# Layer A's output projection on half-precision parts with scanned scales

## The chip, the cores and the metric

The kernel runs on one core of a Trainium2 chip. Its engines have a queue of instructions each: TensorE (PE in the profile, its weight loads apart as PEld), VectorE (DVE), ScalarE (ACT), GpSimd (POOL), and SyncE (SP), which issues the transfers. The metric is the device time of one execution in microseconds; the time before is the median of 3 runs.

## The reference

Two layers of gated attention over 2,048 prompt rows and 64 sample rows (2,112 together, called tokens below), width 1,024. Layer A attends in a window of 192 keys with 16 query heads on 2 key heads and a sink per head; layer B has 16 heads and 576 keys.

```python
def gated_attention_layer(x_p, x_s, ck, cv, norm_g, w_in, q_g, k_g, w_out,
                          n_heads, n_kv, past_chunks, bias_fn, sinks):
    qp, kp, vp, gp = project(x_p, norm_g, w_in, q_g, k_g, n_heads, n_kv)
    op = prompt_band_attention(qp, kp, vp, past_chunks, bias_fn, sinks)
    y_p = x_p + (op * jax.nn.silu(gp)) @ w_out
    ...
for i in range(DEPTH):
    if i % 2 == 0:
        x_p, x_s, k_a_p, v_a_p, k_a_s, v_a_s = gated_attention_layer(...)
    else:
        x_p, x_s, k_b_p, v_b_p, k_b_s, v_b_s = gated_attention_layer(...)
```

`project` normalizes the rows, multiplies by one matrix for q, k, v and the gate, and normalizes q and k per head. What the change touches is `(op * silu(gp)) @ w_out` of the first layer: a product of 2,112 x 1,024 by 1,024 x 1,024.

## The kernel before, in words

**Parts.** A float32 product is made of two parts of each factor, a high one and a low one (what the high one leaves): the kernel multiplies high by high, high by low and low by high, three matmuls. In layer A's output projection the parts are in the format float32r; in layer B's they are half precision (f16), for which both factors are first multiplied by powers of two so that their size fits. Such a scale comes of the largest absolute value of the weights or a bound on the activations. `scan` (L175 to L188) loads pieces of weights (L187) and reduces each to a maximum per partition (L178); it does this for layer B's input weights and output weights only.

**Layer A's attention** (`layer_a`) is a pipeline over 68 items: four groups of four heads (`qd`) by 17 tiles of 128 tokens. An item makes scores, their maxima and exponentials (L1347 on ACT), casts P (L1361) to `values`, transposes it, two heads by DMA and two on TensorE (these are split by L981 on ACT and L982 on DVE, to `ph` and `pl`), multiplies it with the values (L1408), and evacuates (L1495), multiplies by the gate and stores the result (`oga`). Between these steps `filler.to(mark)` puts matmuls of other work on TensorE: first the input projection of the next head group (L758 to L760), and, when that is used up, from about the 59th item, the first units of the output projection.

**Layer A's output projection** is `output_jobs(0, half, ...)`, for two halves of 512 output columns; each half has 8 units of 264 tokens, and a unit 4 blocks (`m`) of 128 columns by 8 chunks (`k`) of 128 rows of the weights. For each `m` and `k` there are three matmuls of 128x264: L2059 (high weights, high activations), L2060 (high, low), L2061 (low, high), 512 of each in all. The block's sum in `pj` (PSUM) is added to the residual by DVE (L2069, the combine), and the rows' squares are summed for the next layer's normalization (`sum_squares`).

The weights of a half come in eight transfers of 128x512 to raw buffers `wraw` (3 of them); the split of each is a cast on ACT to `wh` (L537) and a subtraction on DVE to `wl` (L538). There are 12 buffers `wh` and 12 `wl`. The splits are put in a background list and worked off ahead of their use. The activations of a unit come by four transfers of 128x528 to `xraw` (4 buffers); each is cast by ACT (L639), and POOL makes its low part (L640):

```python
cast = nc.scalar.copy(hi, rv)
nc.gpsimd.tensor_tensor(lo, rv, wide(hi), op=ALU.subtract)
```

High and low parts take four of the seven buffers `xx` for a unit. A unit's activations are prefetched while the unit before it runs. Half 0's units also load one scan each (`scan(j)`).

**What sets the order.** TensorE's order is written out: the program's text with the filler's marks. The order on the other engines is set by a scheduler which sees dependences, buffers and priorities, so that an instruction that becomes possible earlier, or a buffer that is used otherwise, can move others past each other on ACT, DVE, POOL and SP. Each engine then works off its list in order.

**After it.** Layer B (`layer_b`) begins with its input projection and the first items of its attention: copies of q between partitions (L1628 on SP's queue), scores (L1683, L1684), transposes of P (L1748). Its output projection (L2304 to L2308) is half precision with the same 128x264 matmuls.

## Time and the profile before

| | us |
|---|---|
| runs | 2069.28, 2071.61, 2078.48 |
| median | 2071.61 |
| the profiled execution | 2078.12 |
| its span, from the first to the last instruction | 2076.2 |
| layer A's attention up to the last eight items (from the start) | 120 to 616 |
| these eight items, mixed with the output projection | 616 to 686 |
| the rest of layer A's output projection | 686 to 855 |
| layer B | 855 to the end |

The profile's times are counted from the start of the span of one execution. A row of a group gives the line, the engine, the operation, output and input with their shapes, the count, then busy time and the mean of one in ns, and the idle time before them with what ended it. A row of the timeline gives start, duration, and in brackets the idle time before it and its releaser. A row of the windows gives the stretch, its length, then busy time (and count) of PE, PEld, DVE, ACT and POOL, the granted clock, the share of the DMA engines and GB/s.

### The profile page before, as it was taken

The numbers are of one execution on the slowest core, as the hardware profiler recorded it, in microseconds if no ns is written. First come the engines' busy times: TensorE is split into PE (matmuls) and PEld (weight loads), VectorE is DVE, ScalarE is ACT, GpSimd is POOL, SyncE is SP. The second block draws the span as 40 slices with busy tenths as digits, with TensorE's granted clock in tenths as the row PEclk, the third lists the DMA queues.
The fourth block names the chain that finished last, engine by engine and source line by source line (L and its number), as shares of the span: only waits on it lengthen the run. The fifth ranks groups of instructions, "written<-read, shape, count | busy, mean of one in ns | idle before, by whom it ended". The sixth has DMA issues, their size and how long they took to land.

```text
span 2076.2 us, 40598 instructions
## 1 busy us (share of the span) xinstructions
PE 1985.5 (96%) x12718; PEld 1418.1 (68%) x12718; DVE 1432.5 (69%) x4093; ACT 1436.6 (69%) x3568; POOL 1182.6 (57%) x1561
## 2 busy tenths in 40 slices
PE   7899999999999999989999999999999999999899
PEld 6777777777888999745555555555555555557788
DVE  7666767767667555677767676676766767678673
ACT  6877888777788333367768777787867868678430
POOL 5665565544446445577556565665756656566540
PEclk9999999999999999999999999999999999999999
DMA  8877887899766766899889688797997978698753
GB/s 258 255 209 228 221 212 191 236 217 255 194 177 172 214 209 197 281 232 226 226 173 242 168 204 219 174 239 176 200 217 170 233 158 188 149 194 199 200 163 105
DMA packets 600216, 424.64 MB, mean 205 GB/s; under 512 B 403952, under 2 KB 531328, under 8 KB 599968
## 3 DMA queue, kind: packets, MB, share of 16 engines
q1 hardware_dynamic: 600000, 422.06, 80.1%
q8 instruction: 100, 1.64, 0.3%
q14 instruction: 116, 0.95, 0.1%
HBM read 253.14 MB, written 73.43 MB: 157 GB/s over the span
## 4 chain that ended last, share of the span: by engine, by line
PE 50%; DVE 10%; ACT 6%; DMA 5%; issue 5%; POOL 3%; SPq 0%; ACTq 0%; POOLq 0%; DVEq 0%
PE pj L758 9%; PE pj L760 9%; PE pj L759 9%; PE o L1847 4%; PE sb L1683 2%; PE pj L2059 2%; PE pj L2061 2%; PE pj L2060 2%; DMA pt<-values 2%; PE sb L1684 2%; PE pj L2304 2%; PE pj L2308 2%; PE pj L2307 2%; DVE p L1687 1%; PE tp L1011 1%
## 5 line engine op out<-in xcount | busy, mean ns | idle before, releaser
L758 PE MATMUL pj<-wh,xx 128*128 128x512 f16 (+2 forms) x1648 | 643.0, 390 | 17.7 <-DVE pa L852 6.0
L760 PE MATMUL pj<-wh,xx 128*128 128x512 f16 (+2 forms) x1648 | 625.0, 379 | 0.0
L1740 POOL TENSOR_TENSOR values<-p,values 128x640 f16<-128x640 f32 (+4 forms) x256 | 328.4, 1283 | 206.3 <-ACT values L1739 201.9
L759 PE MATMUL pj<-wh,xx 128*128 128x512 f16 x1024 | 388.7, 380 | 1.3 <-DVE wh L545 1.3
L1699 ACT ACTIVATE p<-p,nm 128x640 f32<-128x640 f32 (+5 forms) x264 | 199.6, 756 | 181.3 <-DVE nm L1692 147.7
L1687 DVE CUSTOM_DVE_ANT_0 p<-sb,BT 128x640 f32<-128x640 f32 (+5 forms) x272 | 196.5, 722 | 145.0 <-PE sb L1684 122.3
L640 POOL TENSOR_TENSOR xx<-xraw,xx 128x528 fp32r<-128x528 f32 (+4 forms) x144 | 186.1, 1312 | 96.8 <-ACT xx L639 81.4
L759 PE MATMUL pj<-wl,xx 128*128 128x512 f32 (+1 forms) x624 | 236.1, 378 | 3.0 <-DVE wl L545 3.0
L849 POOL TENSOR_TENSOR f<-f,mhalf 128x4 f32<-128x4 f32 x182 | 187.2, 1028 | 12.1
L1500 POOL TENSOR_TENSOR o<-gt,o 128x256 f32<-128x256 f32 (+1 forms) x132 | 105.7, 801 | 142.0 <-ACT p L1347 71.5
L760 PEld LDWEIGHTS <-xx 128*128 128x128 f16 x1024 | 100.3, 98 | 122.8 <-issue 2.4
L1347 ACT ACTIVATE p<-p,nm 128x257 f32<-128x257 f32 (+2 forms) x272 | 134.4, 496 | 67.3 <-DVE nm L1336 35.3
L1739 ACT CAST values<-p 128x640 f16<-128x640 f32 (+4 forms) x256 | 168.2, 657 | 13.8 <-DMA pt<-values 7.8
L759 PEld LDWEIGHTS <-xx 128*128 128x128 f16 x1024 | 100.3, 98 | 84.5 <-issue 4.9
L758 PEld LDWEIGHTS <-xx 128*128 128x128 f16 x1024 | 100.2, 98 | 82.8 <-ACT sq L827 1.4
L2059 PE MATMUL pj<-xx,wh 128*128 128x264 f32 x512 | 148.4, 290 | 5.3 <-DVE res L2069 2.3
L1847 PEld LDWEIGHTS <-values 128*128 128x128 f16 x1344 | 123.3, 98 | 43.3 <-issue 4.1
L1847 PE MATMUL o<-pt,values 128*128 128x256 f16 (+1 forms) x1344 | 143.7, 255 | 5.9 <-DMA pt<-values 5.9
L2061 PE MATMUL pj<-xx,wl 128*128 128x264 f32 x512 | 145.0, 283 | 0.9 <-DVE wl L538 0.9
L2060 PE MATMUL pj<-xx,wh 128*128 128x264 f32 x512 | 145.7, 284 | 0.0
L758 PEld LDWEIGHTS pj<-wh,xx 128*128 128x128 f32 x624 | 119.7, 192 | 34.9 <-issue 4.6
L760 PEld LDWEIGHTS pj<-wh,xx 128*128 128x128 f32 x624 | 119.1, 191 | 23.3
(369 smaller groups left out, 5060.8 us busy)
## 6 DMA issues: line engine op xcount, KB each, us to landing
xx<-xsb SPq DMA_DIRECT2D x112, 512.0 KB, 4.4
xx<-xsa SPq DMA_DIRECT2D x88, 512.0 KB, 4.8
xraw<-oga SPq DMA_DIRECT2D x64, 264.0 KB, 3.6
xsa<-xx SPq DMA_DIRECT2D x32, 512.0 KB, 4.0
wl<-in_w_in_b_dram SPq DMA_DIRECT2D x64, 256.0 KB, 4.9
wraw<-in_w_in_b_dram SPq DMA_DIRECT2D x56, 256.0 KB, 3.6
xraw<-in_x_dram SPq DMA_DIRECT2D x40, 256.0 KB, 4.3
res<-in_x_dram SPq DMA_DIRECT2D x32, 264.0 KB, 2.9
```

Source lines behind the costliest of these rows:

```text
L640: nc.gpsimd.tensor_tensor(lo, rv, wide(hi), op=ALU.subtract)
L758: nc.tensor.matmul(ps[:n, :C], xh, wh, start=k == 0, stop=False)
L759: nc.tensor.matmul(ps[:n, :C], xh, wl, start=False, stop=False)
L760: nc.tensor.matmul(ps[:n, :C], xl, wh, start=False, stop=k == KC - 1)
L849: nc.gpsimd.tensor_tensor(fv, fv, mhalf[:n, :H], op=ALU.pow)
L1687: mi = nc.vector.tensor_tensor_reduce(out=p[r, :nk], in0=S[r, o : o + nk], in1=b, op0=ALU.add, op1=ALU.min, scale=1.0, scalar=3e38, accum_ ...
L1699: ex = nc.scalar.activation(p[:n, :nk], p[:n, :nk], AF.Exp, scale=-1.0, bias=it.nm[:n, c : c + 1], accum_out=it.sm[:n, c : c + 1],)
L1740: lo = nc.gpsimd.tensor_tensor(two[:, :, 1, :], pv, two[:, :, 0, :], op=ALU.subtract)
L1847: nc.tensor.matmul(it.O[:, h * T + q0 : h * T + q1_], held["VH"][:, kt, h], x, start=kt == kb and not low, stop=kt == tb and low == 1,)
L2059: nc.tensor.matmul(ps[:, :OT], wh, oh, start=k == 0, stop=False)
L2060: nc.tensor.matmul(ps[:, :OT], wh, ol, start=False, stop=False)
L2061: nc.tensor.matmul(ps[:, :OT], wl, oh, start=False, stop=k == KC - 1)
```

## The change

The projection's factors become f16 with scales. For that (1) the 16 pieces of layer A's output weights are scanned during items 20 to 51 (`scales_ahead`, `scan_source`), (2) the gate's weights of each head group, and the cached values, are reduced to maxima (`gate_top`, `load_cache`), as a bound on the activations, (3) the scales are worked out at items 56 to 58 (`first_top`, `first_across`, `first_scales`). (4) Weights are split to a pair in one buffer, of `wh` or, for the last four chunks of a half, of `wl`; half 0 puts all eight splits on the background list at once (`out`). (5) ACT makes the high part of the activations with the scale and scales the raw tile in place; POOL subtracts, and a unit takes two buffers `xx`. (6) The combine multiplies by the inverse scale.

```diff
-    most = const([P, 84], "most")
-    top = const([P, 12], "top")
-    scl = const([P, 9, 4], "scl")
+    most = const([P, 133], "most")
+    top = const([P, 15], "top")
+    scl = const([P, 10, 4], "scl")
...
     S_WO, S_OG, C_O = (scl[:, 8, i : i + 1] for i in range(3))
+    S_WOA, S_OGA, C_OA = (scl[:, 9, i : i + 1] for i in range(3))
...
     def scan_source(i):
+        if i >= 84:
+            return w_o_a[(i - 84) // 8, (i - 84) % 8 // 2, :, i % 2, :]
...
             raw = t("wraw", [P, 512], WB) if keep else t("scan", [P, 512], 1)
-            dst = raw if i < 80 else raw.rearrange("p (e c) -> p e c", e=2)
+            dst = raw if not 80 <= i < 84 else raw.rearrange("p (e c) -> p e c", e=2)
...
+    def gate_top(q, w, *ks):
+        for k in ks:
+            wt, j = w[k]
+            r = nc.vector.tensor_reduce(
+                most[:, 100 + 8 * q + k : 101 + 8 * q + k], wide(wt.h[:, j, 256:512]), axis=AX.X, op=ALU.max,
+                apply_absolute_value=True,
+            )
+            behind(r.ins, bg.anchors[r.ins.engine])
+            scanned.append(100 + 8 * q + k)
+
+    def first_top():
+        largest(12, 84, 100)
+        largest(13, 100, 132)
+        largest(14, 132, 133)
+
+    def first_across():
+        across(12, 15)
+        nc.vector.scalar_tensor_tensor(
+            row[:, 14:15], row[:, 40:41], float(D), row[:, 14:15], op0=ALU.mult, op1=ALU.max
+        )
+        e, r, o = row[:, 48:51], row[:, 52:55], row[:, 56:59]
+        powers(row[:, 12:15], e, r)
+        times(o[:, 0:1], r[:, 0:1], WO)
+        nc.vector.scalar_tensor_tensor(
+            o[:, 1:2], r[:, 1:2], OO, r[:, 2:3], op0=ALU.mult, op1=ALU.mult
+        )
+        nc.vector.scalar_tensor_tensor(
+            o[:, 2:3], e[:, 1:2], 1 / (OO * WO), e[:, 2:3], op0=ALU.mult, op1=ALU.mult
+        )
+        nc.vector.tensor_tensor(o[:, 2:3], o[:, 2:3], e[:, 0:1], op=ALU.mult)
+
+    def first_scales():
+        everywhere(9, row[:, 56:59])
...
-    def load_weights(g, *specs, scale=None):
+    def load_weights(g, *specs, scale=None, apart=False):
...
-                if scale is not None:
+                if scale is not None and not apart:
                     raw = t("wl", [P, 512], WN)
...
                 if scale is None:
                     wh, wl = (t(x, [P, J, C], WN, dt) for x in ("wh", "wl"))
                 else:
-                    both = t("wh", [P, 2, C], WN, dt)
+                    both = t("wl" if apart and i >= WN - 8 else "wh", [P, 2, C], WN, dt)
                     wh, wl = both[:, 0:1], both[:, 1:2]
...
                 hi, lo = (xh[:, :, :T], xh[:, :, T:]) if joint else (xh, xl)
                 if scale is not None:
                     cast = nc.scalar.activation(hi, rv, AF.Identity, scale=scale)
-                    nc.vector.scalar_tensor_tensor(lo, rv, scale, hi, op0=ALU.mult, op1=ALU.subtract)
+                    nc.scalar.activation(rv, rv, AF.Identity, scale=scale)
+                    nc.gpsimd.tensor_tensor(lo, rv, hi, op=ALU.subtract)
...
         load(rvv, vsrc)
+        if not both:
+            nc.vector.tensor_reduce(
+                most[:, 132:133], rv[:, :C], axis=AX.X, op=ALU.max, apply_absolute_value=True
+            )
+            scanned.append(132)
...
             self.jobs, self.n, self.gen, self.done, self.total = [], -1, None, 0.0, 0.0
-        def add(self, prefetch, weights, gen, early=3):
+        def add(self, prefetch, weights, gen, early=3, out=False):
             j = Item()
+            j.out = out
             j.prefetch, j.weights, j.gen, j.early = prefetch, weights, gen, early
             self.jobs.append(j)
 
...
                         nxt.weights()
                 for nxt in self.jobs[self.n + 2 : self.n + 4]:
                     if nxt.weights is not None and nxt is self.jobs[min(self.n + nxt.early, len(self.jobs) - 1)]:
-                        nxt.weights(WN - 8)
+                        nxt.weights(KC if nxt.out else WN - 8)
...
+        def scales_ahead(i):
+            if 20 <= i < 52 and i % 2 == 0:
+                scan(84 + (i - 20) // 2)
+            elif i == 52:
+                scan()
+            q, at = divmod(i, 17)
+            if 0 <= q < 4 and 1 <= at < 5:
+                gate_top(q, st.w[q], 2 * at - 2, 2 * at - 1)
+            if i == 56:
+                first_top()
+            elif i == 57:
+                first_across()
+            elif i == 58:
+                first_scales()
+                held["out"] = True
+
         def pipeline():
             N = len(items)
             for i in range(-3, N + 1):
...
                 if i + 3 < N:
                     end = max(items[i + 3].mark, c0 + AVG_A)
                 filler.attending = i >= 0
+                scales_ahead(i)
                 if 0 <= i < N:
                     scores(items[i])
                     if i == N - 1:
...
             if st.emit is None:
+                assert layer or held["out"]
                 (st.w,), _, st.emit = load_weights(
-                    None, ((w_o_a, w_o_b)[layer][half], 512), scale=(None, S_WO)[layer]
+                    None, ((w_o_a, w_o_b)[layer][half], 512), scale=(S_WOA, S_WO)[layer], apart=layer == 0
                 )
             st.emit(*m)
 
...
-                st.x[j] = x = load_act(og[layer], o, OT, dt=(F32R, F16)[layer], scale=(None, S_OG)[layer])
+                st.x[j] = x = load_act(og[layer], o, OT, dt=F16, scale=(S_OGA, S_OG)[layer])
                 if half == 0 and j == 0:
                     st.res = residual(0, 0)
                 return x
...
                         nc.tensor.matmul(ps[:, :OT], wl, oh, start=False, stop=k == KC - 1)
-                    if layer:
-                        nc.vector.scalar_tensor_tensor(
-                            rv[:, m % 2], ps[:, :OT], C_O, rv[:, m % 2], op0=ALU.mult, op1=ALU.add
-                        )
-                    else:
-                        nc.vector.tensor_tensor(rv[:, m % 2], ps[:, :OT], rv[:, m % 2], op=ALU.add)
+                    nc.vector.scalar_tensor_tensor(
+                        rv[:, m % 2], ps[:, :OT], (C_OA, C_O)[layer], rv[:, m % 2], op0=ALU.mult, op1=ALU.add
+                    )
+                    if not layer:
                         if half == 0 and m == 0:
                             scan(j)
                         if half and j < 2 and m % 2 == 0:
...
                     yield 3 * OT / 2400
 
             filler.total += 96 * OT / 2400
-            filler.add(prefetch, weights if j == 0 else None, gen)
+            filler.add(prefetch, weights if j == 0 else None, gen, out=half == 0)
 
         for j in range(NO):
             add_unit(j)
```

Lines after the change: L2059, L2060 and L2061 become L2121, L2122 and L2123; L537 and L538 become L571 and L572; L639 becomes L669 (high part) and L670 (in place); L640 becomes L671; L2069 becomes L2126; L178 and L187 become L181 and L190.

TensorE at the first matmuls of the output projection, before: `wh` and `wl` are the weights' parts, `xx` the activations', `values` and `ph` the operands of an item's product.

```order
L1011 MATMUL tp_9048<-ident,G_8873 128x128 x2
L2059 MATMUL pj_9081<-xx_8810,wh_8507 128x264
L2060 MATMUL pj_9081<-xx_8810,wh_8507 128x264
L2061 MATMUL pj_9081<-xx_8810,wl_8508 128x264
L1408 LDWEIGHTS values_106
L1408 MATMUL o_9085<-ph_9014,values_106 128x256
L1408 LDWEIGHTS values_106
```

And after:

```order
L1054 MATMUL tp_9142<-ident,G_8985 128x128 x2
L2121 LDWEIGHTS wh_8607
L2121 MATMUL pj_9177<-xx_8920,wh_8607 128x264
L2122 LDWEIGHTS wh_8607
L2122 MATMUL pj_9177<-xx_8920,wh_8607 128x264
L2123 LDWEIGHTS wh_8607
L2123 MATMUL pj_9177<-xx_8920,wh_8607 128x264
L1452 LDWEIGHTS values_106
L1452 MATMUL o_9181<-ph_9108,values_106 128x256
L1452 LDWEIGHTS values_106
```

The order of the matmuls is the same; each now has a weight load of its own in the list, and the low weights are in the same buffer as the high ones.

ACT around the 58th item, from the cast of the transposed P's high part (`ph`) to the evacuations of the next projection (`pa`, `pb`), before:

```order
L981 CAST ph_8749<-sa_8751 128x512
L1347 ACTIVATE p_8704,sm_8697<-p_8704,nm_8696 128x257
L639 CAST xx_8810<-xraw_8802 128x528
L1361 CAST values_106<-p_8704 128x2x256
L639 CAST xx_8813<-xraw_8804 128x528
L1279 ACTIVATE q_1900_8775<-tp_8770,qf 64x2x128 x2
L1485 ACTIVATE gt_8778<-tp_8770,sva 128x256
L783 ACTIVATE pa_8786<-pj_8744,rms_102 64x256
L783 ACTIVATE pb_8787<-pj_8744,rms_102 64x256
L639 CAST xx_8816<-xraw_8806 128x528
```

And after:

```order
L1019 CAST ph_8856<-sa_8858 128x512
L1391 ACTIVATE p_8808,sm_8801<-p_8808,nm_8800 128x257
L669 ACTIVATE xx_8920<-xraw_8912,scl 128x528
L669 ACTIVATE xx_8920<-xraw_8914,scl 128x528
L1405 CAST values_106<-p_8808 128x2x256
L669 ACTIVATE xx_8927<-xraw_8916,scl 128x528
L669 ACTIVATE xx_8927<-xraw_8918,scl 128x528
L670 ACTIVATE xraw_8912<-xraw_8912,scl 128x528
L1323 ACTIVATE q_1919_8885<-tp_8880,qf 64x2x128 x2
L1546 ACTIVATE gt_8888<-tp_8880,sva 128x256
L670 ACTIVATE xraw_8914<-xraw_8914,scl 128x528
```

Where three casts of activations (L639) stood between these rows, four scaled ones (L669) and two scalings in place (L670) stand now, in front of the cast of P (L1361, now L1405) and of the evacuations that follow.

DVE where half 0 of the projection gives way to half 1: weight splits (L538, later L572), combines (L2069, later L2126), before, at the end of half 0:

```order
L2069 TENSOR_TENSOR res_10400<-pj_10461,res_10400 128x264
L2007 TENSOR_TENSOR BT<-p_10488 128x72
L2007 TENSOR_TENSOR row_9210<-p_10488 128x192
L2069 TENSOR_TENSOR res_10492<-pj_10494,res_10492 128x264
L538 TENSOR_TENSOR wl_10431<-wraw_10136,wh_10430 128x512
L538 TENSOR_TENSOR wl_10440<-wraw_10145,wh_10439 128x512
L538 TENSOR_TENSOR wl_10447<-wraw_10158,wh_10446 128x512
L2069 TENSOR_TENSOR res_10492<-pj_10520,res_10492 128x264
L538 TENSOR_TENSOR wl_10458<-wraw_10434,wh_10457 128x512
```

And after, at the sixteenth of half 0's 32 combines:

```order
L572 SCALAR_TENSOR_TENSOR wl_10536<-wraw_10240,scl,wl_10536 128x512
L572 SCALAR_TENSOR_TENSOR wl_10544<-wraw_10248,scl,wl_10544 128x512
L2126 SCALAR_TENSOR_TENSOR res_9907<-pj_9909,scl,res_9907 128x264
L2068 TENSOR_TENSOR BT<-BT,p_9895 128x264
L181 TENSOR_REDUCE most<-scan_10092 128x1
L2070 TENSOR_TENSOR BT<-BT,p_9895 128x264
L2126 SCALAR_TENSOR_TENSOR res_9907<-pj_9952,scl,res_9907 128x264
L572 SCALAR_TENSOR_TENSOR wl_10550<-wraw_10260,scl,wl_10550 128x512
L2068 TENSOR_TENSOR BT<-p_9979 128x264
L2126 SCALAR_TENSOR_TENSOR res_9982<-pj_9984,scl,res_9982 128x264
L572 SCALAR_TENSOR_TENSOR wl_10560<-wraw_10539,scl,wl_10560 128x512
L2126 SCALAR_TENSOR_TENSOR res_9982<-pj_10010,scl,res_9982 128x264
```

The last of half 1's eight splits stands ahead of half 0's sixteenth combine, where before four of them stood about the last ones.

SP where layer B begins: the loads of x and of weights (`xraw`, `wraw`), stores (`xsb`, `out_dram`), and the first copies of q, before:

```order
L391 DMA BT<-skew 128x256
L651 DMA xsb<-xx_11910 128x2048
L620 DMA xraw_12049<-x_99 128x2x256
L1628 DMA q_2399_11967<-q_2399_11967 64x256 x2
L620 DMA xraw_12051<-x_99 128x2x256
L651 DMA xsb<-xx_11924 128x2048
L620 DMA xraw_12053<-x_99 128x2x256
L187 DMA wraw_12116<-in_w_in_b_dram 128x512
L417 DMA out_dram<-in_ck_a_rows_dram 16x512
```

And after:

```order
L428 DMA BT<-skew 128x256
L657 DMA xraw_12167<-x_99 128x2x256
L689 DMA xsb<-xx_12040 128x2048
L657 DMA xraw_12169<-x_99 128x2x256
L190 DMA wraw_12232<-in_w_in_b_dram 128x512
L454 DMA out_dram<-in_ck_a_rows_dram 16x512
L1689 DMA q_2369_12083<-q_2369_12083 64x256 x2
L1809 DMA_TRANSPOSE pt_12216<-values_11903 128x2x128
```

The first copies of q come behind five transfers that followed them before.

## The prediction

> **What bounds the kernel now.** I read the page's first two parts, then the windows by stage, then the timeline of TensorE in the stage that the change touches, and last the idle times of TensorE there.
>
> ```profile
> span 2076.2 us, 40598 instructions
> PE 1985.5 (96%) x12718; PEld 1418.1 (68%) x12718; DVE 1432.5 (69%) x4093; ACT 1436.6 (69%) x3568; POOL 1182.6 (57%) x1561
> ```
>
> TensorE is busy for 96% of the span, every other engine for 69% or less. So the time follows the number of matmuls, their spacing, and the places where TensorE waits. The stages (start and end, then busy time by engine):
>
> ```profile
> 120.00:616.00 496.00, 481.90 (x2830) 390.22 (x2829) 350.02 (x1159) 399.67 (x1099) 263.47 (x441) 0.99 0.81 212
> 616.00:686.00 70.00, 66.40 (x492) 59.90 (x491) 53.35 (x150) 57.29 (x150) 46.64 (x60) 1.00 0.70 185
> 686.00:855.00 169.00, 162.72 (x1329) 161.09 (x1328) 87.98 (x158) 56.54 (x94) 80.95 (x69) 1.00 0.69 211
> 855.00:2077.00 1222.00, 1173.66 (x7506) 722.74 (x7503) 858.66 (x2361) 834.29 (x1997) 719.97 (x887) 1.00 0.82 196
> ```
>
> The columns that matter are the first (PE), third (DVE), fourth (ACT) and the granted clock. From 120 to 616 us layer A attends; from 616 to 686 the last eight items of attention share the engines with the first units of the output projection; from 686 to 855 the projection runs alone; after that comes layer B. In the projection alone TensorE is busy for 162.72 of 169 us and ACT for a third. In the mixed stage ACT is busy for 57.29 of 70 us, nearly as full as TensorE.
>
> **The change, part by part.** First the spacing of the matmuls. The two pairs of rows are the first and last of 85 float32 matmuls in a row in the projection, and of 92 half-precision ones of the same 128x264 shape in layer B's projection:
>
> ```profile
> 719.74 0.29 PE L2060 MATMUL pj<-xx,wh 128*128 128x264 f32 x1
> ...
> 729.92 0.28 PE L2060 MATMUL pj<-xx,wh 128*128 128x264 f32 x1
> ```
>
> ```profile
> 2034.76 0.28 PE L2308 MATMUL pj<-xx,wx 128*128 128x264 f16 x1
> ...
> 2044.99 0.28 PE L2304 MATMUL pj<-xx,wx 128*128 128x264 f16 x1
> ```
>
> 84 steps in 10.18 us are 121.2 ns each; 91 steps in 10.23 us are 112.4 ns. The change gains 8.8 ns on each matmul of the projection. Lines 2059, 2060 and 2061 hold 512 each, 1536 together, so 13.5 us at most. They divide so (L2059 alone):
>
> ```profile
> 616.00:686.00 70.00, 25.41 (x84) 15.75 (x84) 1.00 0.70 185
> 686.00:855.00 169.00, 122.98 (x429) 80.42 (x429) 1.00 0.69 211
> ```
>
> 3 x 429 matmuls after 686 us gain **11.3 us**; 3 x 84 in the mixed stage would gain 2.2 us if TensorE still set the pace there. The separate weight load that each now has is in the 112.4 ns already, as the rows of layer B have it too.
>
> The Trainium skill ("TensorE: Matmul & The Clock Gate", section "Back-to-back issue gap") gives a warm gap of N/2.4 + 2.5 ns, whatever the type: 112.5 ns for 264 columns, an estimate by that page. The half-precision rows agree; the float32 rows, at 121.2 ns, do not. By the rule for both kinds this term would be nothing; the rows decide.
>
> Second, the boundary between the halves. TensorE waits there for the last weight splits:
>
> ```profile
> 756.13 0.39 PE L2059 MATMUL pj<-xx,wh 128*128 128x264 f32 x1 [1.44 <-ACT wh L537]
> 757.51 0.39 PE L2061 MATMUL pj<-xx,wl 128*128 128x264 f32 x1 [0.88 <-DVE wl L538]
> ```
>
> Since both parts of a chunk now fit one buffer, half 1 needs no buffer that half 0 still holds; the order shows all eight splits ahead of the sixteenth combine of half 0, where before the last four stand at its end. I count **2.3 us** gained, at least 0 if another wait for the same loads takes its place.
>
> Third, the mixed stage. Before, TensorE stands idle in it twice:
>
> ```profile
> 641.26 0.27 PE L1408 MATMUL o<-pl,values 128*128 128x256 f16 x1 [2.00 <-DVE pl L982]
> 647.67 0.36 PE L2059 MATMUL pj<-xx,wh 128*128 128x264 f32 x1 [1.60 <-ACT QS L1292]
> ```
>
> That is 3.6 us. The first comes from weight splits that stand ahead of pl L982 on DVE; these move some 35 us earlier, so it should go. What is late next is ACT. Its own steps, from rows of several like instructions:
>
> ```profile
> 681.17 1.66 ACT L537 CAST wh<-wraw 128x512 fp32r<-128x512 f32 x3
> 689.55 2.23 ACT L639 CAST xx<-xraw 128x528 fp32r<-128x528 f32 x4
> 1925.11 2.61 ACT L2206 ACTIVATE xx<-xraw,scl 128x528 f16<-128x528 f32 x4
> ```
>
> With the last one's duration taken off (0.62, 0.63 and 0.73 us), a weight cast steps by 0.52 us, an activation cast by 0.53 and the scaled one by 0.63. ACT now does two scaled operations for each chunk: the high part, and the chunk scaled in place. The trace has no in-place one; between the square of the same tile (0.53 or so) and a full second 0.73 I take 0.63. Moreover its queue runs further ahead: two buffers serve a unit instead of four, and between the same two marks (the copies of o that end items 59 and 67) the order has 20 casts and 20 in-place scalings against 15 casts, and 3 weight activations against 7. That adds 40 x 0.63 + 3 x 0.62 - 15 x 0.53 - 7 x 0.52 = **15.3 us** to 57.29: 72.6 us of work in a stage that lasted 70. ACT runs its queue in order, and exponentials, evacuations and parts of P stand behind the scalings.
>
> The Trainium skill ("Perfetto Trace Analysis", section "Optimizing Scalar/DVE Operations") says that about half the overhead in a profiled latency overlaps with the next instruction. The rows agree (0.73 long, 0.63 apart); adding the 40 at their length, without that rule, the stage would hold 4 us more.
>
> How much reaches TensorE is not in the trace. From below: ACT's work hides altogether, and the 3.6 us and the 2.2 us are gained, -5.8. From above: ACT keeps all its idle time, +15.3. With no idle at all it is +2.6; with the idle share of the fullest stretch,
>
> ```profile
> 640.00:650.00 10.00, 7.14 (x59) 6.76 (x59) 8.00 (x24) 9.57 (x28) 8.64 (x11) 1.00 0.77 207
> ```
>
> 96% busy, 72.6 us become 75.9, +5.9. I take the middle of these two, **+4 us**.
>
> Fourth, the scans. 16 reductions of 128x512 and one small one, 32 of 128x256 and some 25 tiny operations go to DVE, 16 loads of 256 KB to SP's queue.
>
> ```profile
> L845 DVE TENSOR_REDUCE f<-sq 128x4 f32<-128x256 f32 x182 | 75.0, 412 | 16.5 <-ACT sq L797 7.6 <-ACT sq L806 7.5
> L178 DVE TENSOR_REDUCE most<-wraw 128x1 f32<-128x512 f32 x76 | 51.5, 678 | 0.3
> L2069 DVE TENSOR_TENSOR res<-pj,res 128x264 f32<-128x264 f32 x64 | 27.3, 429 | 57.0 <-PE pj L2061 56.9
> L2296 DVE SCALAR_TENSOR_TENSOR res<-pj,scl,res 128x264 f32<-128x264 f32 x48 | 23.4, 489 | 25.4 <-PE pj L2308 25.3
> ```
>
> 17 x 0.68 + 32 x 0.41 + about 3 are 28 us of DVE. In 120:616 DVE is idle for 146 us, and the waits of TensorE on DVE are few:
>
> ```profile
> PE o L1408 <- DVE pl L982: 3.1, 7, 0.5
> ```
>
> Behind a reduction on DVE stand the score minima, and ACT's exponentials wait for those; the next matmul that needs them is an item later. Behind a scan's load on SP stand the copies of q and the transposes of P. Nearly all is covered; I take **+2 us**, with 0 and 28 as ends. The combine, 489 instead of 429 ns, 64 times, is 3.8 us of DVE beside TensorE, with 81 us of idle time to cover it: nothing. The low parts stay on POOL with the same two inputs and a half-precision output; the nearest rows are L640 itself and one that writes half precision:
>
> ```profile
> L640 POOL TENSOR_TENSOR xx<-xraw,xx 128x528 fp32r<-128x528 f32 x64 | 88.1, 1405 | 60.9 <-ACT xx L639 45.9 <-DMA x<-res 8.3 <-issue 6.4
> L1740 POOL TENSOR_TENSOR values<-p,values 128x640 f16<-128x640 f32 (+4 forms) x256 | 328.4, 1283 | 206.3 <-ACT values L1739 201.9
> ```
>
> 1405 ns for 528 columns, 1283 for 640 or fewer: by either, 64 of them change by 0 to -8 us on an engine that is idle for a third or more of both stages, so nothing for TensorE. Three transposes and one small matmul for the scales cost TensorE under 1 us, which I leave out.
>
> Fifth, layer B's start. From about its third unit every engine's order is the same row for row, so it moves as a block. Ahead of that one move matters: the first copies of q stand on SP's queue ahead of five more transfers before the change and behind them after it (the second row below is the fifth).
>
> ```profile
> 875.23 1.33 SPq L1628 DMA_DIRECT2D q<-q  x2
> ...
> 880.69 0.56 SPq L417 DMA_DIRECT2D out_dram<-in_ck_a_rows_dram  x1
> ```
>
> ```profile
> q<-q SPq DMA_DIRECT2D x218, 32.0 KB, 3.4
> ```
>
> ```profile
> 881.70 0.27 PE L1683 MATMUL sb<-KA,q 128*128 128x256 f16 x1
> ```
>
> With 3.4 us from issue to landing they came by 878.6, 3.1 us before the scores that read them. Behind 880.69 + 0.56 they would be issued 6 us later and land at 884.65, 2.95 us late, and TensorE's order is fixed, so it would wait. I take **+3 us** because I see nothing that would bring the five transfers forward; the ends are 0 (they come earlier, since some of SP's waits go) and +6 (the scores had no slack at all).
>
> The sum: -11.3 - 2.3 + 4 + 2 + 3 = **-4.6 us**. The profiled execution took 2078.1 us (span 2076.2 and 1.9 around it), so 2073.5; it lies 6.5 us above the median of the runs shown, 2071.6, so for a median I forecast **2067.0**.
>
> **The rivals.** (a) ACT's extra work hides: exponentials have several microseconds of slack between scores and transposes. For it: TensorE had only two waits in the stage. Against: 72.6 us do not fit 70. It gives -5.8 instead of +4, and 1 for the scans: -15.4, 2056. (b) ACT keeps its idle time, since each scaling lets POOL and DVE start later: +15.3 instead of +4, +6.7 in all, 2078. For it: in its group POOL waits 45.9 us for L639, which becomes the slower pair L669 and L670; against: ACT was 96% busy where it was needed. (c) Slower: the DVE reductions in attention pass into the items. Price 28 us, place 120:616. It decides once 6.6 of them reach TensorE (the 4.6 gained in all, and the 2 counted); with all of them the sum is +21.4, 2093. Against it: 146 us idle there and 3.1 us of waits. (d) The change does not give its rate: layer A's matmuls stay at 121 ns because something else paces them. Then 11.3 go, +6.7, 2078.
>
> For (d) speaks only that POOL needs 4 x 1.4 us for a unit and ACT 8 x 0.63; a unit's 96 matmuls at 112.4 ns last 10.8, so both fit.
>
> **How the numbers follow.** Forecast 0.44, (a) 0.27, (b) 0.14, (c) 0.08, (d) 0.07. Runs before range over 9 us, and 0.5%, 10.4 us, is about what a measurement here tells from no change. The forecast's own spread (ACT 0 to +8, layer B 0 to +6) is -11.6 to +2.4; with the noise of the runs a fifth of it is over 0.5% faster, with nearly all of (a): 0.35. (c) with over 17 of its 28 us, and the upper edge of (b) and (d), are over 0.5% slower: 0.10; the rest, 0.55, is within.
>
> ```profile
> 699.22 0.39 PE L2059 MATMUL pj<-xx,wh 128*128 128x264 f32 x1 [1.85 <-DVE res L2069]
> ```
>
> This wait comes of a scan on DVE and may go with (a). The range holds (a) with some noise and without it, down to 2051, and (b) and (d) up to 2082; outside are most of (c) and a little on each side.
>
> **What would show it.** Rows of 128x264 half-precision matmuls 112 ns apart from about 690 us to the start of layer B, and that stretch about 14 us shorter: first two terms. No wait of TensorE at the half's boundary: second. ACT busy over 95% in the last eight items of attention, and those items longer than before by some 4 us: third; wrong if they are shorter. Items before 616 us as long as before within 2 us: fourth. The first scores of layer B waiting some 3 us for their q: fifth. The prediction is wrong if layer B's stretch changes by more than that, or if TensorE's idle time appears behind POOL's low parts.

## The result and the profile after

| | before, us | after, us | ratio, 95% interval |
|---|---|---|---|
| first set (4 and 4 runs) | 2070.53 | 2090.24 (2089.32 to 2094.04) | 1.0091 [1.0062, 1.0119] |
| second set (23 and 6 runs) | 2072.49 | 2092.99 (2086.92 to 2094.73) | 1.0100 [1.0075, 1.0125] |
| profiled execution (span) | 2078.12 (2076.2) | 2090.94 (2088.8) | |

The change costs about 20 us; forecast was a gain of 4.6, with a range that ended at 2082. One of the 23 executions of before, 3002.85 us at a granted clock of 0.63, counts in the median and not in the ratio. The two profiled executions are only 12.8 us apart: that of before was some 6 us above its median, and the table below has before 5.4 us longer in a stretch of layer B (B 0-12) where the change alters no operation.

To see where the time went, the spans are cut at the same events in both: the copies that end an item of attention (L1495, after the change L1556) and the last matmul of layer A's projection. Each column is the length of a stretch in us. "A" stands for layer A's items, "B" for layer B's; the scales are worked out between items 55 and 59, and the third stretch is the mixed one.

| | A 0-55 | A 55-59 | A 59-66 | projection | to B 0 | B 0-12 | rest |
|---|---|---|---|---|---|---|---|
| before | 508.0 | 32.8 | 62.8 | 176.2 | 54.3 | 207.8 | 956.1 |
| after | 508.8 | 36.5 | 67.9 | 179.8 | 59.4 | 202.4 | 957.2 |
| after, second profile | 510.9 | 35.9 | 67.8 | 181.3 | 59.8 | 203.0 | 955.0 |

"Projection" runs from the last but one item's end to the last matmul. There the forecast gained 13.6 us; the profiles lose 3.6 and 5.1. The half-precision matmuls do run at the rate that was counted. The timeline of TensorE after the change, first and last of 91 in a row:

```profile
824.30 0.27 PE L2121 MATMUL pj<-xx,wh 128*128 128x264 f16 x1
...
834.43 0.28 PE L2121 MATMUL pj<-xx,wl 128*128 128x264 f16 x1
```

90 steps in 10.13 us are 112.6 ns. What goes against it are waits. TensorE's waits from 690 to 870 us (releaser, us in all, times, longest), after the change:

```profile
PE pj L2121 <- DVE res L2126: 12.1, 7, 3.9
PE o L736 <- DVE BT L2070: 3.0, 3, 1.5
PE o L736 <- DVE scrow L221: 1.9, 1, 1.9
```

The same view of before, from 683 to 857 us:

```profile
PE pj L2059 <- DVE res L2069: 2.3, 2, 1.8
PE o L698 <- DVE BT L2009: 1.7, 2, 1.0
PE pj L2059 <- ACT wh L537: 1.4, 1, 1.4
PE pj L2061 <- DVE wl L538: 0.9, 1, 0.9
```

The waits for the weight splits at the boundary of the halves (last two rows) are gone, as forecast; the wait for the combine (L2069, now L2126) has grown from 2.3 to 12.1 us. In all TensorE waits 17.0 us for 6.3. Behind some of these waits it also ran some 40 matmuls at half rate, 4.3 us more (last section). These add up: 11.3 gained by the rate, 10.7 and 4.3 lost, 3.7 us longer for 3.6 measured. DVE, which makes the combine, waits itself, after the change:

```profile
DVE res L2126 <- DMA res<-in_x_dram: 15.9, 6, 4.4
DVE most L181 <- DMA scan<-in_w_in_b_dram: 12.0, 5, 6.8
```

It waits for the loads of the residual and of layer B's scans, that is for SP's queue; before, it never waited for the residual, and for the scans 7.2 us. And ACT, from 690 to 860 us, in before (first row) waited for TensorE to free the activations' buffers, and waits now for the raw activations first (second row; before, it waited for those once, 2.5 us) and less for TensorE (third row):

```profile
ACT xx L639 <- PE pj L2061: 26.6, 10, 3.5
```

```profile
ACT xx L669 <- DMA xraw<-oga: 18.0, 14, 3.4
ACT xx L669 <- PE pj L2123: 14.9, 6, 3.7
```

So the flow has turned round in part: TensorE set the pace, now the supply of activations often does. The chain of waits after the change from 700 to 745 us says so in its first row (shares of this stretch), and its pieces show the way of a tile:

```profile
by line: DMA xraw<-oga 34.8%; DMA x<-res 10.4%; issue 10.3%; DMA scan<-in_w_in_b_dram 9.7%; ACT xraw L670 6.7%; POOL xx L671 5.3%; ACT xx L669 4.9%; PE pj L2121 3.8%; SPq L657 3.5%; PE pj L2122 3.4%; PE pj L2123 3.4%; DVE most L181 1.5%; SP
...
712.90 0.73 ACT xraw L670
713.62 0.07 issue
713.69 1.20 POOL xx L671
714.91 6.08 DMA xraw<-oga
...
728.20 4.70 DMA x<-res
732.95 0.37 SPq L2085
733.32 0.05 issue
733.37 0.47 SPq L657
733.84 0.05 issue
733.89 4.38 DMA scan<-in_w_in_b_dram
738.29 0.69 DVE most L181
```

A raw tile is scaled in place (L670), GpSimd subtracts (L671), and only then may the next tile be loaded into it. Further on, SP's queue stands for a store of the residual (x<-res), behind it come a residual load (L2085), a tile (L657) and the scan; the scan's reduction stands on DVE ahead of the combine for which TensorE waits until 740.23.

In the mixed stretch ACT is as full as was forecast. The windows from 626 to 676 us (PE, PEld, DVE, ACT, POOL), before and then after:

```profile
626.00:676.00 50.00, 46.40 (x350) 41.99 (x350) 39.01 (x116) 42.26 (x115) 33.50 (x46) 1.00 0.66 167
```

```profile
626.00:676.00 50.00, 41.80 (x311) 33.72 (x310) 30.77 (x99) 49.09 (x118) 35.12 (x47) 1.00 0.57 148
```

ACT goes from 42.26 to 49.09 of 50 us, TensorE from 46.40 to 41.80.

### The profile page after: what moved, and what is told of

Same layout as the page of the kernel before. It is cut to its first block, busy times and chain, and to the rows that moved or that the text cites. A ratio compares the mean times of both kernels' runs of the same rounds, so it can differ in the third digit from the quotient of the medians.

```text
span 2088.8 us, 40708 instructions
## 1 busy us (share of the span) xinstructions
PE 1977.5 (95%) x12723; PEld 1381.2 (66%) x12723; DVE 1442.3 (69%) x4155; ACT 1481.5 (71%) x3632; POOL 1170.2 (56%) x1561
## 4 chain that ended last, share of the span: by engine, by line
PE 57%; DVE 13%; ACT 10%; DMA 10%; issue 6%; POOL 4%; SPq 1%; ACTq 0%; DVEq 0%; POOLq 0%
PE pj L796 11%; PE pj L798 11%; PE pj L797 11%; PE o L1908 4%; DMA pt<-values 3%; PE sb L1744 2%; PE sb L1745 2%; PE tp L1054 2%; PE pj L2364 2%; PE pj L2368 1%; PE pj L2367 1%; PE pj L2121 1%; PE pj L2122 1%; PE pj L2123 1%; DVE p L1748 1%
## 5 line engine op out<-in xcount | busy, mean ns | idle before, releaser
L886 POOL TENSOR_TENSOR f<-f,small 128x4 f32<-128x4 f32 x182 | 38.1, 210 | 166.0 <-DVE f L883 148.0
L797 PEld LDWEIGHTS pj<-wl,xx 128*128 128x128 f32 x624 | 119.1, 191 | 17.4 <-DVE wl L582 3.0
L671 POOL TENSOR_TENSOR xx<-xraw,xx 128x528 f16<-128x528 f32 x64 | 78.4, 1238 | 86.2 <-ACT xraw L670 83.8
L1556 ACT COPY o<-o 64x256 f32<-64x256 f32 (+1 forms) x264 | 96.2, 364 | 37.9 <-PE o L1908 27.7
```

The lines of the kernel that those rows point to most:

```text
L797: nc.tensor.matmul(ps[:n, :C], xh, wl, start=False, stop=False)
L1556: nc.scalar.copy(o1v[rows], Ov[64:128, :, hh, :])
```

## The experiments

Two theories stood first for the projection. Theory 1: the two residual buffers (load, two combines, store) set the pace. Theory 2, later A: the raw activation tiles' way with its second pass. The diffs are against the changed kernel unless said otherwise; each result stands beside the kernel before on the same chip, and a table at the end has the stretches of all. The stretches of a run are those of one execution. In e13, which alters nothing in the projection, it took 176.3 us where the change's two profiles have 179.8 and 181.3, so a difference of up to some 5 us in one stretch is not certain.

**e1: without the scaling in place.**

```diff
                     cast = nc.scalar.activation(hi, rv, AF.Identity, scale=scale)
-                    nc.scalar.activation(rv, rv, AF.Identity, scale=scale)
                     nc.gpsimd.tensor_tensor(lo, rv, hi, op=ALU.subtract)
```

> Leaves out the scaling of the raw activations in place (64 operations of ACT, 0.63 us each); the low parts are then formed from unscaled tiles and mean nothing. Theory 1 (the residual's two buffers set the pace of the projection: load, two combines, store, and the next load waits for the store on SP's queue): only the mixed stage gains, 6 to 9 us, and TensorE's waits on the combine after 690 us stay above 10 us; about 2083. Theory 2 (ACT's second pass holds the raw tiles longer, so their loads hold up SP's queue and the residual and scan loads behind them): the waits on the combine after 690 us fall below 5 us as well, about 2070.

Measured: 2077.8 us (12 runs), ratio 1.0029 [1.0013, 1.0045], some 15 us below the change's 1.0100 where Theory 2 wanted 20. The projection takes 165.7 us, 14 less than in the change's first profile, and TensorE's wait for the combine there is down to

```profile
PE pj L2120 <- DVE res L2125: 4.6, 5, 1.9
```

4.6 us. Its granted clock from 690 to 855 us is 1.00, so the half-rate matmuls are gone too. The mixed stretch gains only 2.2. By the waits Theory 2 holds: the second pass costs most where ACT was idle for half the time. What this run does not tell apart is the longer way of the tile and the longer list of ACT.

**e2: four residual buffers. e3: the same in the kernel before.**

```diff
-            rv = t("res", [P, 2 * OT], 2).rearrange("p (k s) -> p k s", k=2)
+            rv = t("res" if c % 4 == 0 else "more", [P, 2 * OT], 2).rearrange("p (k s) -> p k s", k=2)
```

> Four residual buffers in layer A's output projection instead of two (two tiles that are otherwise used in layer B's output alone). Theory 1: TensorE's waits on the combine after 690 us fall from 12 us to under 4, the low clock around 740 us goes with them, about 2076; the mixed stage stays 8 to 9 us longer than before. Theory 2: the waits stay within 3 us of what they are, about 2090.

> The kernel before with the same four residual buffers. Theory 1: at 121 ns a matmul two buffers nearly kept up, so it gains 0 to 3 us (TensorE waits 2.3 us on the combine there before). Theory 2: no change. If it gains 8 us or more, the residual was a bound before the change too, and the comparison of the other runs has to start from it.

Measured: e2 2092.72 us (6 runs), 1.0085 [1.0060, 1.0109], against 1.0100 for the change: no gain that can be told. Its profile is of its fastest execution (2082.26); there the projection is 4 to 6 us shorter (175.4) and TensorE waits 7.2 us for the combine, between what the two theories wanted. e3 2078.42 us (12 runs), 1.0025 [1.0010, 1.0041]: no gain either, rather a loss. Theory 1 falls as the main cause; the residual is one customer of SP's queue among others.

**e4: constant scales, no scans. e7: scans kept, scales constant.** Constants stand in both for the worked-out scales. In e4 the scans, the reductions of the gate weights and of the cached values go too:

```diff
-            if 20 <= i < 52 and i % 2 == 0:
-                scan(84 + (i - 20) // 2)
...
             if i == 56:
-                first_top()
-            elif i == 57:
-                first_across()
-            elif i == 58:
-                first_scales()
+                for c, v in enumerate((2.0 ** 14, 2.0, 2.0 ** -15)):
+                    nc.vector.tensor_scalar(scl[:, 9, c : c + 1], nsink[:, 0:1], 0.0, v, op0=ALU.mult, op1=ALU.add)
                 held["out"] = True
```

> The change with constant scales: no scans of the output weights, no reductions of the gate weights or the cached values, no working out of the scales (16 loads, 49 reductions and some 25 small operations, 3 transposes and 1 small matmul left out). Theory 1 and 2: only items up to the 58th change, by 2 us of TensorE's waits at the two scale transposes and some 2 us elsewhere: 2086. Rival (the 28 us of DVE work of the scans pass into the items): 8 us or more faster, under 2082.

> Scans and reductions stay, but the scales are constants (no working out, no transposes for it). If TensorE's two waits for the scales at items 56 to 58 are the cost, it takes all that leaving out the scans took, about 8 us below the change; if the 16 loads and 49 reductions are, 2 us or less.

Measured: e4 2082.17 us (12 runs), 1.0038 [1.0023, 1.0053]; e7 2086.02 us (6 runs), 1.0068 [1.0041, 1.0095]. The interval of e7 overlaps that of the change, so its 7 us are not certain; that of e4 does not, and it lies some 13 us below the change, more than the 8 us from which the expectation let the reductions pass into the items. In both profiles the stretch from item 55 to 59 is at the kernel before's 32.8 us, where every run that works out the scales has 35.4 to 36.5: 3 to 4 us for it. TensorE's two waits in the change's timeline are 2.1 us of that:

```profile
581.90 0.49 PE L213 MATMUL tp<-ident,top 128*1 128x128 f32 x3 [1.07 <-DVE q L1330]
591.66 0.35 PE L229 MATMUL tp<-scrow,ones 1*128 1x3 f32 x2 [1.07 <-DVE q L1330]
```

The scans themselves are harder to price. Items 0 to 55 take 507.6 to 515.3 us in the profiles with them and 502.9 and 504.0 without, yet 508.0 and 512.8 in the two kernels that never had them. So leaving them out is worth some 8 us in the mean (511.2 and 503.5), and having added them costs some 1 (511.2 and 510.4). The order of the other engines' work, which the scheduler settles anew for each kernel, may move as much; that no run shows, and it stays open.

**e5: the change again. e6: both left out** (e1's and e4's diffs together).

> The changed kernel again, as the control of this set: about 16 us above the kernel before (2090 where that has 2074), since runs of one kernel range over some 14 us and the earlier sets had other numbers of runs.

> Both leave-outs together: no scaling in place and constant scales without scans, so the low activation parts mean nothing. What is left is the half-precision rate, the moved weight splits and the pairs of buffers. If the two costs are separate (in-place about 12 us, scans about 8), 20 us below the change, 2070 where the kernel before has 2074. If they share one wait, only 12 us below, 2078. By the prediction's gains alone (11.3 + 2.3 + 2.2 + 3.6) it would be 19 us below the kernel before, 2055.

Measured: e5 as in the first table. e6 2069.44 us (12 runs), 0.9986 [0.9970, 1.0003]: some 23 us below the change, so the two costs are nearly separate, but no gain over the kernel before that can be told. With neither cost the projection is 167.1 us, 9.1 below before; the gain is given back at the start of layer B (60.2 for 54.3) and in the mixed stretch (64.9 for 62.8). The prediction's gains alone would have made it 2055.

**e8: low parts by DVE from the raw tile. e10: the scaling in place on DVE.** First e8, then e10:

```diff
-                    nc.scalar.activation(rv, rv, AF.Identity, scale=scale)
-                    nc.gpsimd.tensor_tensor(lo, rv, hi, op=ALU.subtract)
+                    nc.vector.scalar_tensor_tensor(lo, rv, scale, hi, op0=ALU.mult, op1=ALU.subtract)
```

```diff
-                    nc.scalar.activation(rv, rv, AF.Identity, scale=scale)
+                    nc.vector.tensor_scalar(rv, rv, scale, None, op0=ALU.mult)
```

> The low parts by one operation of DVE from the raw tile with the scale, as layer B's projection makes them: no scaling in place on ACT, none of the 64 subtractions on GpSimd, 64 operations of DVE more (0.7 to 0.9 us each, 50 us). Theory (the raw tile's way through ACT twice and GpSimd holds its buffer and with it SP's queue): 12 us below the change as without the scaling, 2078. Rival (DVE, which also has the combines and the squares' sums, becomes the late one): TensorE's waits on the combine stay above 10 us, 2088 or more.

> The change with the scaling in place on DVE instead of ACT: the raw tile goes through as many passes as in the change, but ACT has one of them. Theory A: the projection alone stays within 4 us of the change (176 to 182 us between the last item of attention and the last matmul). Theory B: it is 8 to 14 us shorter, as without the scaling. In the last eight items of attention both expect 2 to 4 us less, since ACT is full there; in all 2090 by A, 2078 by B.

Measured: e8 2081.44 us (12 runs), 1.0042 [1.0025, 1.0058]; projection 171.3, mixed 63.9. e10 2087.98 us (6 runs), 1.0082 [1.0057, 1.0107]; projection 180.4, mixed 63.2. Freeing ACT of the second pass (e10) mends the mixed stretch and leaves the projection as long as it was; TensorE then waits for the combine ten times, for shorter:

```profile
PE pj L2121 <- DVE res L2126: 10.4, 10, 1.6
PE o L736 <- DVE BT L2070: 9.8, 5, 6.2
```

Taking the pass off ACT and out of the tile's way (e8) mends both. So in the mixed stretch most of the price is ACT's time, though e1 frees ACT as much and gains 2.2 there. For the projection e10 gave the number of Theory A by another way, and so does not refute Theory B: its raw tiles no longer come late, ACT waits for TensorE again as in before, and it is DVE, with the pass on it, that TensorE waits for (both rows above). ACT's waits in e10:

```profile
ACT xx L669 <- PE pj L2123: 34.0, 9, 10.9
ACT xx L669 <- DMA xraw<-oga: 5.1, 5, 2.1
```

**e9: six raw tiles. e11: conversions not more than a unit ahead. e12: e8 with six raw tiles.** First e9 (and e12), then e11:

```diff
-                raw = t("xraw", [P, 2 * OT], XB)
+                raw = t("more", [P, 2 * OT], 2) if scale is not None and c < 2 else t("xraw", [P, 2 * OT], XB)
```

```diff
         def place(c):
+            if scale is not None:
+                return t("xx", [P, 8 * OT], XN, dt)[:, : 4 * T]
```

> The change with six raw activation tiles instead of four (the first two chunks of each unit in two tiles that are otherwise used in layer B's output). Theory A (four raw tiles are too few once each is held through two passes of ACT and one of GpSimd): TensorE's waits in the projection alone fall from 11 us to 5 or less and the stage is 8 to 14 us shorter, about 2080 where the change has 2093. Theory B (ACT's list in order: the second passes stand ahead of the squares, DVE waits for the squares and the combine stands behind): the stage shortens by less than 3 us, 2091.

> The change with a buffer of its own for each of a unit's four activation tiles, so that four of seven are used by a unit as before and the conversions cannot run more than a unit ahead. Theory A: within 4 us of the change, 2089 to 2095. Theory C (the conversions run too far ahead, so that their loads stand on SP's queue ahead of the residual's and the scans'): the projection alone is 6 to 12 us shorter, about 2083.

> The low parts by DVE from the raw tile, with six raw tiles. Theory A: most of what is left of the waits for raw tiles goes, 2 to 5 us better than with four, about 2077; it does not reach the kernel before (2073), since the working out of the scales (some 4 us) and the later start of layer B (some 5 us) stay.

Measured: e9 2089.53 us (6 runs), 1.0078 [1.0050, 1.0107]; e11 2081.78 us (12 runs), 1.0042 [1.0025, 1.0059]; e12 2079.37 us (12 runs), 1.0038 [1.0021, 1.0054]. With six tiles (two for the first two tiles of a unit, four for its other two) the projection is 172.8, 7 to 8.5 us shorter, a little under what A wanted, and TensorE's wait for the combine halves:

```profile
PE pj L2121 <- DVE res L2126: 6.0, 4, 3.0
```

but the mixed stretch is 2.5 longer (70.4), with the same 32 conversions on ACT as in the change, so why is not shown; in all no gain can be told. e11 contradicts A, which expected nothing, and bears out the time of C: 174.5 in the projection, at the lower edge of what C wanted, and 63.8 in the mixed stretch, although a tile goes through as many passes as in the change. Between the ends of items 59 and 66 its profile has 28 conversions on ACT, the change's 32; it also has 15 more of the projection's matmuls there, so 1.7 us of the shorter projection are only moved. So how far ahead the conversions stand counts; that the number of raw tiles counts as well, e9's projection suggests. e12 gains nothing over e8 that can be told, where A wanted 2 to 5 us.

**e13: the scales' place in the item. e14: e12 with that place. e15: e8 with e11's buffers and that place.**

```diff
                 filler.attending = i >= 0
-                scales_ahead(i)
...
                 filler.to(c0 + 0.3 * (end - c0))
+                scales_ahead(i)
```

> The change with the scans, reductions and the scales' working out issued at three tenths of an item instead of at its start (before the turns of q rather than before the scores). If the cost between the 55th and the 59th item (3.7 us in each run that works out the scales, 0 in each that doesn't) is TensorE's wait for the transpose bank that the last turn of q still holds, it falls to under 1 us, and the time by 3 to 5 us, to about 2088; if it is the operations themselves, nothing changes, 2092.

> Low parts by DVE from the raw tile, six raw tiles, and the scales' place of the run above. If the terms add, 4 us below the run without the moved scales, 2075 where the kernel before has 2073: no gain over the kernel before, since layer B's later start (some 5 us) stays.

> Low parts by DVE, four raw tiles, a buffer of its own for each activation tile (conversions not more than a unit ahead), and the scales' place moved. If running ahead is a cost of its own beside the raw tiles' way, 3 to 5 us below the run above, 2071; if both remedy one wait, the same as that run or up to 3 us above it.

Measured: e13 2092.44 us (6 runs), 1.0098 [1.0082, 1.0115]; e14 2080.60 us (11 runs), 1.0040 [1.0026, 1.0053]; e15 2080.38 us (9 runs), 1.0044 [1.0028, 1.0059]. In e13 the two waits of 1.07 us are gone, but items 55 to 59 still take 35.6 us. The guess about the bank was right about the wait and wrong about the cost; what the cost is stays open. e14 and e15, expected at 2075 and 2071 if the remedies add up, are no better than e12: they do not add up. Only e6, which leaves both out, is level with the kernel before.

| | A 0-55 | A 55-59 | A 59-66 | projection | to B 0 | ratio to before |
|---|---|---|---|---|---|---|
| after (e5) | 510.9 | 35.9 | 67.8 | 181.3 | 59.8 | 1.0100 |
| e1 no scaling in place | 515.3 | 36.0 | 65.6 | 165.7 | 59.1 | 1.0029 |
| e2 four residuals | 510.4 | 36.1 | 67.9 | 175.4 | 56.2 | 1.0085 |
| e3 before, four residuals | 512.8 | 32.8 | 63.9 | 177.0 | 52.8 | 1.0025 |
| e4 no scans | 502.9 | 32.9 | 67.7 | 180.5 | 60.5 | 1.0038 |
| e6 neither | 504.0 | 32.9 | 64.9 | 167.1 | 60.2 | 0.9986 |
| e7 constant scales | 512.7 | 32.8 | 67.7 | 178.8 | 60.4 | 1.0068 |
| e8 low parts by DVE | 507.6 | 36.1 | 63.9 | 171.3 | 60.5 | 1.0042 |
| e9 six raw tiles | 510.8 | 36.2 | 70.4 | 172.8 | 59.8 | 1.0078 |
| e10 scaling on DVE | 510.8 | 36.3 | 63.2 | 180.4 | 60.2 | 1.0082 |
| e11 a buffer each | 513.6 | 36.2 | 63.8 | 174.5 | 58.1 | 1.0042 |
| e12 e8 and six tiles | 509.8 | 36.4 | 65.2 | 170.5 | 58.3 | 1.0038 |
| e13 scales moved | 510.4 | 35.6 | 67.8 | 176.3 | 59.5 | 1.0098 |
| e14 e12, scales moved | 512.8 | 35.7 | 66.1 | 171.5 | 56.7 | 1.0040 |
| e15 e8, e11, scales moved | 511.1 | 35.4 | 60.4 | 176.1 | 59.8 | 1.0044 |

## Why the prediction was wrong

**The rate (-11.3)** was right as a rate: 112.6 ns in the rows above. But it was booked as time. The step that failed is the sentence under rival (d), that GpSimd's and ACT's work for a unit "both fit" into the 10.8 us of its matmuls. It added up each engine's busy time and took the spare time for cover. Left out was the time from the load into a raw tile to the end of the subtraction that frees it, and what stands behind it on ACT's list and SP's queue. In the change's trace that time is 10.8 us on average over the 44 tiles loaded after 690 us (issue of the load to the end of L671), and 1.2 us more pass until the next load into the tile is issued. Four tiles make a unit, so units come every 12.0 us where the matmuls need 10.8: the prediction saw half of ACT idle, and the supply was late.

Such a mean is not a floor, since it holds waiting: in before it is 11.8 us, of which 5.0 lie between the landing and the cast, while ACT, among other things, waits for TensorE (26.6 us in the row above). The pass itself shows behind the high part: from its end to the start of the subtraction go 2.5 us in the change, 0.8 in e1 and 0.9 in before. With the pass gone (e1) the projection drops to 165.7, 10.5 us under before and near the forecast's 162.6. That the second pass on ACT costs this is shown; how it does, by the tile's way or by ACT's list in order, is in part argued, since e10 loads DVE instead and e11 is faster with the same passes.

**The boundary (-2.3)**: the weights are no longer waited for, as forecast; the time was lost again in the combine's wait, which is the zero end of that term.

**The mixed stage (+4)** was right: 67.9 and 67.8 us for 62.8, +5, with ACT at 98% from 626 to 676 us. e10 and e8, which free ACT, give it back.

**The scans (+2)**: items 0 to 55 at +0.8 and +2.9 agree with it against before, but the kernels without scans are some 8 us shorter there, which stays open. The scales' working out was put at under 1 us and left out; it costs 3 to 4. TensorE's two waits for them are not the reason, since e13 is without them and as slow there.

**Layer B's start (+3)**: +5.1 and +5.5, and 2 to 6 us in every version of the change, so the size was about right by luck and the reason wrong. The scores wait for q no longer than before (2.71 for 2.83 us). New is a wait of the transposes on DVE, in the change's timeline:

```profile
885.94 0.66 PE L1054 MATMUL tp<-ident,pa 128*128 128x128 f32 x2 [2.58 <-DVE pa L961]
886.39 0.63 PE L796 MATMUL pj<-wh,xx 128*128 128x512 f16 x1
886.82 0.63 PE L797 MATMUL pj<-wh,xx 128*128 128x512 f16 x1
...
889.56 0.38 PE L798 MATMUL pj<-wh,xx 128*128 128x512 f16 x1
889.78 0.38 PE L796 MATMUL pj<-wh,xx 128*128 128x512 f16 x1
```

The chain of waits there runs over GpSimd's low parts of layer B's activations (L678) to pa L961. That was only read off the trace; no run moved it.

Rival (c) named nearly the measured time, 2093, but its 28 us did not come: items 0 to 55 are 1 to 3 us longer than before. Rival (d) let something else pace the projection and so came nearest to the mechanism, but it took the matmuls to stay at 121 ns and priced it at no gain. No rival had the supply of activations, though "TensorE's idle time appears behind POOL's low parts" was listed as what would make the prediction wrong.

## What to carry to other kernels

Speeding up the engine that sets the pace is worth only what its supply can follow: for each ring of buffers work out how long one buffer is held, from the issue of its load to the operation that frees it, and divide by the number of buffers. Leave out the waiting for the engine that sets the pace, which a measured hold contains, and leave room for transfers that come late. Spare busy time of the engines in between is no cover. A second pass over a tile lengthens that hold (here from 0.8 to 2.5 us between two steps), and loads that stand behind in the issuing queue come late with it. A change that lets conversions run further ahead can put them into a stage where their engine is full (e11).

## What the runs showed of the hardware

Behind some waits TensorE runs at half its rate for a while. In the change's chain behind the wait that ends at 740.23 us the matmuls of 264 columns stand 220 ns apart, and the granted clock there is 0.50 (the third figure from the end of the windows' row):

```profile
740.64 0.22 PE pj L2122
740.86 0.22 PE pj L2123
741.08 0.22 PE pj L2121
```

```profile
741.00:742.00 1.00, 1.00 (x7) 0.66 (x6) 0.00 (x0) 1.00 (x3) 0.16 (x1) 0.50 0.89 261
```

The 40 such steps after 690 us, up to 746 and from 787 to 790, are 4.3 us on top of the waits. The rows at 886.39 show the same for 512 columns (430 ns apart, later 215). It is not fixed by the length of the wait: in the same trace the first of these waits was followed by no slow step, and the second, which is shorter, by the slow ones from 787:

```profile
778.48 0.29 PE L2121 MATMUL pj<-xx,wh 128*128 128x264 f16 x1 [2.90 <-DVE res L2126]
...
786.04 0.58 PE L736 MATMUL o<-ones,BT 128*128 128x2 f32 x4 [1.88 <-DVE scrow L221]
```

In the second profile of the change, behind a wait of 4.31 us that ended at 741.42, three steps were at the full rate before the slow ones began. The Trainium skill ("TensorE: Matmul & The Clock Gate", section "What's actually happening") puts half rate behind an idle window of some 3.4 us that runs freely. That fits slow steps that do not begin with the end of the wait, and two of the stretches at 0.50 last about 3.4 us (from 787 and from 886). But the waits that ended at 786.04 and at 885.94 were 1.88 and 2.58 us, shorter than that window.

Executions of one kernel ranged over some 14 us (before: 2065 to 2079 in 29 runs), so a few runs can't tell 5 us apart.
